# A hybrid encoder on one Trainium2 core: ten raw-weight buffers in the down-projection's first halves, and one more seven-product unit per layer

## Chip, cores and metric

The kernel runs on one core of one Trainium2 chip. The metric is the device time of one execution in microseconds (us); lower is better. A core has five engines that matter here: TensorE (PE; its weight loads are shown apart, as PEld) for matmuls, VectorE (DVE), ScalarE (ACT) and GpSimd (POOL) for elementwise work, and SyncE (SP), which issues nearly all the loads. Each engine works through its own instructions in order. All data are float32.

## The reference

An encoder of two layers over 256 positions of width 2048. Layer 0 has grouped-query attention with rotary positions, layer 1 three groups of dilated sliding-window attention. Either is followed by a gated feed-forward block with a depthwise convolution of width 3, which is what the change is about:

```
def conv_ffn(h, w_up, conv_w, conv_b, w_down):
    u = h @ w_up                                   # [256, 2048] @ [2048, 11264]
    u = lax.conv_general_dilated(u, ...) + conv_b  # depthwise, over positions, width 3
    gate, val = jnp.split(u, 2, axis=-1)           # 5632 columns each
    return (jax.nn.silu(gate) * val) @ w_down      # [256, 5632] @ [5632, 2048]

for i in range(DEPTH):                             # DEPTH = 2
    h = h + mixer(rms_norm(h, mix_norm[i]))
    h = h + conv_ffn(rms_norm(h, ffn_norm[i]), w_up[i], conv_w[i], conv_b[i], w_down[i])
return rms_norm(h, final_norm)
```

## The kernel before

**Split products.** To keep float32 accuracy on PE, each operand is split into a rounded high part and the rest: for a weight tile `raw`, ACT makes `wh` (a rounding copy) and DVE makes `wl = raw - wh`. A product is three matmuls, high by high, high by low and low by high (lines 160 to 162). The activations are the stationary operand, the weights stream through.

**An ordinary step, `feed`.** The weights lie in DRAM as blocks of 512 rows by 512 columns. `feed` takes one such block (a `kg`, 1 MB): it issues two loads of 512 KB (line 150), each into a raw buffer of 128 x 1024, splits each (lines 171 and 172) into a pair of buffers wh and wl, and issues 24 matmuls of 128x512, 12 per raw buffer. The split is given a priority 60 instructions ahead of its place (`AHEAD`), so that it runs ahead of the matmuls; which instruction of an engine comes when is fixed when the program is built.

**The seven-product unit, `fast_unit`.** For two column blocks n0 and n1 at the same kg, the work is a product of 2 x 2 blocks: two halves of the positions by two halves of the 512 rows, times those by two column blocks. Eight block products are done as seven (a scheme of the Strassen kind), 42 matmuls in place of 48 (lines 212 to 214). For that DVE makes four sums of weights (line 204), and seven weight tiles are split (lines 205 and 206) in place of four. The sums of activations are made once per kg and kept in `picks`. The accumulators of seven products are then folded into the four wanted ones: in the up-projection by lines 594 to 604, eight operations of 128x512 on DVE and one copy on ACT.

**Buffers.** `raw_tile` hands out raw buffers: four (`NRAW`) with tag raw, and, where `extra` is set, every third one from two further buffers with tag raw2, six in all. `new_split` hands out wh and wl: four pairs (`NHL`), and while `more` is set (in the up-projection behind a half's first pair) every third one from h0 and h1, two tiles of 8 KB per partition that hold the residual at other times and are parked in DRAM during most of the feed-forward block. SP issues the loads in order; a load waits until its raw buffer has been read by DVE.

**The feed-forward block, `ffn`.** The 5632 gate and 5632 value columns are worked in 11 pairs of a 512-column gate block and a value block, in two halves: pairs 0 to 5, then the down-projection of those (this document calls it the first half of the down-projection), then pairs 6 to 10 and the rest. A pair runs over four kgs. Pairs listed in `UP` (2, 4, 6 and 8) go through `up_pair`, with kg 0 as a seven-product unit in the order `UP_ORDER`; the others through `project`, gate first. The picks for kg 0 are made behind pair 0 (and for the second half from sums begun in the down-projection). Behind a pair come evacuation (ACT, line 539), a transposition (DVE line 427, POOL and ACT line 679), convolution (lines 659 and 667), silu, the product (703) and the split of the result (744, 745, or `combined` for kgs 1 and 2, which the down-projection takes in seven-product units). These are generators that `step` advances between the matmuls of `feed`; for pairs in UP the gate's generator goes into the list `beside`, which is advanced at other places of `feed` than the list `pending`.

**The down-projection's first half.** `pair` runs twice, for column blocks (0, 1) and (2, 3), each over six kgs in the order 0, 0, 3, 3, 4, unit 1, 4, 5, unit 2, 5: eight feeds and two units. The sums of weights for its units go into the u tiles of the convolution (`spot`), and results are added to the parked residual in DRAM.

Of the kernel before, what the change touches and what calls it, by code (L numbers as in the profile page):

```python
# [8 lines left out]
F32 = mybir.dt.float32  # L9
# [5 lines left out]
P = 128  # L15
# [7 lines left out]
SCALE = 128.0 ** -0.5  # L23
NRAW, NHL = 4, 4
AHEAD = 60
UP = 2, 4, 6, 8
MIX = (0, 1), (0, 2), (1, 1), (1, 2)
MIX_ORDER = (1, 0), (2, 0), (3, 0), (1, 1), (2, 1), (0, None), (3, 1)
EVEN = range(0, 16, 2)
# [7 lines left out]
def tile_encoder(ctx: ExitStack, tc: tile.TileContext, x, xT, w_a, w_ao, q_gain, k_gain, w_b, w_bo,  # L37
# [5 lines left out]
    hpool = ctx.enter_context(tc.tile_pool(name="hpool", bufs=1))  # L43
    spool = ctx.enter_context(tc.tile_pool(name="spool", bufs=1))
# [13 lines left out]
    h = {}  # L58
# [4 lines left out]
    def nm(s):  # L63
        uid[0] += 1
        return f"{s}_{uid[0]}"
# [58 lines left out]
            if len(pending) > keep:  # L124
                step()

    extra, count = [None], [0]

    def raw_tile():
        count[0] += 1  # L130
        if extra[0] and count[0] % 3 == 0:
            pool, tags = extra[0]
            tags.append(tags.pop(0))
            return pool.tile([P, 2, 512], F32, tag=tags[0], name=nm("raw"), bufs=2 if len(tags) == 1 else 1)
        return spool.tile([P, 2, 512], F32, tag="raw", name=nm("raw"), bufs=NRAW)
# [214 lines left out]
    def project2(w, n0, n1, lhs, kgs, late, first_done, hook=None, cuts=(), drained=()):  # L350
        a0, a1 = new_acc(), new_acc()
        cuts = (0, *cuts, len(kgs) - late, len(kgs))
        for c0, c1 in zip(cuts, cuts[1:]):
            part, end = range(c0, c1), c1 == len(kgs)
            if end:
                drain()
                for gen in drained:
                    start(gen())
            for accs, n in ((a0, n0), (a1, n1)):
                for i in part:  # L360
                    kg = kgs[i]
                    mid = hook and hook(n == n0, kg)
                    feed(accs, lhs, kg, w[n, kg], i == 0, i == len(kgs) - 1,
                         pieces=4 if hook and i < 2 else 2 if hook else 1, mid=mid)
                if end and n == n0:
                    first_done(a0)
        return a1
# [239 lines left out]
    def ffn(l, hT, ss_in, cw, g_next, last, side=None):  # L607
        with tc.tile_pool(name=nm("fpool"), bufs=1) as fp:
# [63 lines left out]
            def turned(s, u, at_once=False):  # L672
                quad = quad_tile(fp, "quad", 2)
                for m in range(2):
                    quad_T(quad, slice(m, 8, 2), s[:, m])

                def move(i, put):
                    q, c = QC[i]
                    put(u[32 * c:32 * c + 32, :, :, 32 * q:32 * q + 32],  # L679
                        quad[32 * q:32 * q + 32, c].rearrange("p (j m) t -> p j m t", m=2))  # L680

                for i in range(0, 16, 2):
                    move(i, nc.gpsimd.tensor_copy)
                if not at_once:
                    yield
                for i in range(1, 16, 2):
                    move(i, partial(nc.scalar.activation, func=AF.Copy))

            def gate_gen(accs, blk, value):
                s = evac_scaled(fp, accs, rstd, 1)  # L690
                yield
                yield from turned(s, blk[1])
                if value is not None:
                    for _ in range(1 if blk[0] not in UP else 4 if value[5] // 4 - 1 in fast else 3):
                        yield
                    with tc.issue_after(evac[0].ins):
                        nc.scalar.activation(value[3], value[3], AF.Silu)
                    yield from product(value)
# [6 lines left out]
            def value_gen(accs, blk, gate, last):  # L705
# [10 lines left out]
                yield from turned(s, blk[1])  # L716
                wait = 5 if last is None or gate[0] + 1 in UP else 4 if gate[0] in UP else 2
                if gate[0] + 1 in UP and last is not None and last[5] // 4 in fast:
                    for _ in range(wait):
# [70 lines left out]
            for hf, (p0, p1) in enumerate(HALVES):  # L790
# [5 lines left out]
                for p in range(p0, p1):  # L796
# [5 lines left out]
                    def gate_done(accs, gate=gate, last_value=last_value):  # L802
                        gen = gate_gen(accs, gate, last_value)
                        if gate[0] in UP:
                            next(gen)
# [7 lines left out]
                    if p == 0:  # L813
                        va = project2(w_up[l], 0, NPAIR, hT, kgs, 1, gate_done, None, (), [first])
                    elif p in UP:
                        va = up_pair(w_up[l], (p, NPAIR + p), hT, UP_ORDER, picks, junk, st_tile, gate_done)
# [92 lines left out]
                both = {kg: [(kg, 0), (kg, 1)] for kg in rest}  # L909
                f0, f1 = ([(kg, None)] for kg in fast)  # L910
                if hf == 0:
                    for ns in (0, 1), (2, 3):
                        if ns[0] == 2:
                            early = [fp.tile([P, 4, NT], F32, tag=t, name=nm(t)) for t in ("cg", "cv")]
                            start(sums_begun(hT, 0, *early, 4))
                        pair(wd, ns, slots, both[0] + both[3] + [(4, 0)] + f0 + [(4, 1), (5, 0)] + f1 + [(5, 1)], spot, folds,
                             None, 3 * (ns[0] == 0), ready)
                    continue
                accs = new_acc()
                for kg in range(np_):  # L920
# [725 lines left out]
```

## Time and profile before

| | |
|---|---|
| median of three timed runs | 2223.69 us (2222.29 to 2225.51) |
| profiled execution | 2221.27 us |
| its span, first to last instruction | 2219.5 us |
| PE busy | 2206.1 us (99%), 9933 matmuls |
| DVE busy | 1809.3 us (82%) |
| ACT busy | 1522.7 us (69%) |
| POOL busy | 543.5 us (24%) |
| granted clock of PE | 0.999 |
| read from HBM, written to it | 436.54 MB, 13.73 MB |

A row of the timeline has the start, the length, the engine, the line of the kernel, the operation, what it writes and reads, the shapes and the count; a bracket behind it says how long the engine stood idle before it and what ended that. A row of a group has the count, then the busy time, the mean length in ns of one, the idle time of the engine just before its members, and what ended it. Matmuls are pipelined: the length of one is longer than the distance to the next.

Where things lie in this execution: layer 0's pairs 0 to 5 from 257 to 516 us, its first half of the down-projection from 516 to 642; in layer 1 from 1505 to 1764 and from 1764 to 1891.

### The profile page before, as it was taken

How to read it: one execution, taken by the hardware profiler on the slowest of the kernel's cores; microseconds unless marked ns; L12 is line 12 of the kernel's file. 1: busy time of each engine (PE TensorE's matmuls, PEld its weight loads, DVE VectorE, ACT ScalarE, POOL GpSimd, SP SyncE). 2: the span in 40 equal slices, each digit the busy share in tenths (PEclk: the TensorE clock that was granted, in tenths of full speed). 3: DMA queues.
4: the chain of work that ended last, by engine and by line, in shares of the span. 5: the costliest groups of instructions: out<-in, count | busy, mean ns of one | idle time of the engine just before them, and what ended most of it. 6: DMA issues, size and time to landing. Idle time of an engine off the chain costs nothing.

```text
span 2219.5 us, 29025 instructions
## 1 busy us (share of the span) xinstructions
PE 2206.1 (99%) x9933; PEld 1829.4 (82%) x9933; DVE 1809.3 (82%) x2279; ACT 1522.7 (69%) x2328; POOL 543.5 (24%) x809
## 2 busy tenths in 40 slices
PE   9999999999999999999999999999999999999998
PEld 7888888888888888888888888888888888888887
DVE  6877768898887897978876878688798898879887
ACT  7666777787457787677756775567777855577754
POOL 3343221321002121041354216003222200212211
PEclk9999999999999999999999999999999999999999
DMA  8666765565767566666566555667565567756754
GB/s 302 193 221 201 240 205 181 192 200 188 216 209 237 184 203 224 206 202 199 180 202 197 171 184 187 192 203 242 168 219 190 189 202 212 238 173 209 255 191 142
DMA packets 129510, 452.19 MB, mean 204 GB/s; under 512 B 14665, under 2 KB 18505, under 8 KB 128337
## 3 DMA queue, kind: packets, MB, share of 16 engines
q1 hardware_dynamic: 123056, 429.05, 58.7%
q0 software_dynamic: 6016, 20.98, 3.9%
q8 instruction: 78, 1.28, 0.2%
q14 instruction: 72, 0.58, 0.1%
q10 hardware_dynamic: 288, 0.30, 0.0%
HBM read 436.54 MB, written 13.73 MB: 203 GB/s over the span
## 4 chain that ended last, share of the span: by engine, by line
PE 94%; DVE 2%; DMA 1%; issue 1%; POOL 1%; ACT 1%; SPq 0%; DVEq 0%; POOLq 0%; ACTq 0%
PE acc L161 27%; PE acc L160 27%; PE acc L162 27%; PE ps L213 2%; PE ps L212 2%; PE ps L214 2%; PE acc L213 2%; PE acc L214 2%; PE acc L212 2%; DVE wl L172 1%; DMA raw<-in_w_a_dram 1%; DMA raw<-in_w_down_dram 0%; PE ps L393 0%; PE ps L392 0%; DVE wl L206 0%
## 5 line engine op out<-in xcount | busy, mean ns | idle before, releaser
L172 DVE TENSOR_TENSOR wl<-raw,wh 128x1024 fp32r<-128x1024 f32 (+1 forms) x612 | 747.4, 1231 | 208.8 <-ACT wh L171 205.0
L171 ACT ACTIVATE wh<-raw 128x1024 fp32r<-128x1024 f32 (+1 forms) x612 | 633.5, 1044 | 277.6 <-PE acc L162 178.9
L160 PE MATMUL acc<-wh,xh 128*128 128x512 f32 x1632 | 636.7, 391 | 0.8 <-ACT wh L171 0.8
L161 PE MATMUL acc<-wl,xh 128*128 128x512 f32 x1632 | 636.1, 390 | 0.8 <-DVE wl L172 0.8
L162 PE MATMUL acc<-wh,xh 128*128 128x512 f32 x1632 | 634.8, 389 | 0.0
L679 POOL COPY u<-quad 32x256 f32<-32x256 f32 x352 | 223.5, 635 | 663.5 <-DVE quad L427 645.4
L161 PEld LDWEIGHTS acc<-wl,xh 128*128 128x128 f32 x1632 | 306.5, 188 | 64.4 <-DVE wl L172 2.7
L160 PEld LDWEIGHTS acc<-wh,xh 128*128 128x128 f32 x1632 | 306.5, 188 | 64.0 <-ACT wh L171 1.2
L162 PEld LDWEIGHTS acc<-wh,xh 128*128 128x128 f32 x1632 | 306.4, 188 | 63.9
L160 PE MATMUL acc<-wh,a 128*128 128x512 f32 x720 | 280.9, 390 | 0.0
L161 PE MATMUL acc<-wl,a 128*128 128x512 f32 x720 | 280.2, 389 | 0.0
L162 PE MATMUL acc<-wh,a 128*128 128x512 f32 x720 | 279.7, 389 | 0.0
L205 ACT ACTIVATE wh<-raw 128x1024 fp32r<-128x1024 f32 x128 | 135.7, 1060 | 116.0 <-PE acc L162 92.0
L679 ACT ACTIVATE u<-quad 32x256 f32<-32x256 f32 x352 | 147.8, 420 | 38.9 <-DVE quad L427 34.5
L206 DVE TENSOR_TENSOR wl<-raw,wh 128x1024 fp32r<-128x1024 f32 x128 | 154.2, 1222 | 12.0 <-ACT wh L205 11.4
L162 PEld LDWEIGHTS acc<-wh,a 128*128 128x128 f32 x720 | 135.1, 188 | 28.5 <-DVE a L378 0.2
L160 PEld LDWEIGHTS acc<-wh,a 128*128 128x128 f32 x720 | 135.2, 188 | 27.6
L161 PEld LDWEIGHTS acc<-wl,a 128*128 128x128 f32 x720 | 135.2, 188 | 27.4
L172 DVE TENSOR_TENSOR w<-raw,w 128x1024 fp32r<-128x1024 f32 x88 | 110.3, 1253 | 41.6 <-ACT w L171 41.6
L160 PE MATMUL acc<-w,xh 128*128 128x512 f32 x352 | 136.9, 389 | 0.0
L162 PE MATMUL acc<-w,xh 128*128 128x512 f32 x352 | 136.9, 389 | 0.0
L161 PE MATMUL acc<-w,xh 128*128 128x512 f32 x352 | 136.9, 389 | 0.0
(358 smaller groups left out, 3066.5 us busy)
## 6 DMA issues: line engine op xcount, KB each, us to landing
raw<-in_w_up_dram SPq DMA_DIRECT2D x352, 512.0 KB, 4.8
raw<-in_w_down_dram SPq DMA_DIRECT2D x176, 512.0 KB, 4.7
raw<-in_w_b_dram SPq DMA_DIRECT2D x144, 512.0 KB, 4.7
raw<-in_w_bo_dram SPq DMA_DIRECT2D x48, 512.0 KB, 4.3
raw<-in_w_a_dram SPq DMA_DIRECT2D x40, 512.0 KB, 4.7
raw<-in_w_ao_dram SPq DMA_DIRECT2D x32, 512.0 KB, 4.7
raw<-in_w_a_dram SPq DMA_DIRECT2D x16, 256.0 KB, 5.8
away<-h POOLq DMA_DIRECT2D x4, 1024.0 KB, 5.8
```

Source lines behind the costliest of these rows:

```text
L160: nc.tensor.matmul(accs[m], xh, wh[:, j, :], start=st, stop=False)
L161: nc.tensor.matmul(accs[m], xh, wl[:, j, :], start=False, stop=False)
L162: nc.tensor.matmul(accs[m], xl, wh[:, j, :], start=False, stop=sp)
L171: nc.scalar.activation(wh[:, c], r[:, c], AF.Copy)
L172: newest[0] = nc.vector.tensor_tensor(wl[:, c], r[:, c], wh[:, c].bitcast(F32), ALU.subtract)
L205: nc.scalar.activation(wh, r, AF.Copy)
L206: newest[0] = nc.vector.tensor_tensor(wl, r, wh.bitcast(F32), ALU.subtract)
L212: nc.tensor.matmul(acc[q], a, wh[:, j], start=st, stop=False)
L213: nc.tensor.matmul(acc[q], a, wl[:, j], start=False, stop=False)
L214: nc.tensor.matmul(acc[q], b, wh[:, j], start=False, stop=sp)
L679: put(u[32 * c:32 * c + 32, :, :, 32 * q:32 * q + 32], quad[32 * q:32 * q + 32, c].rearrange("p (j m) t -> p j m t", m=2))
```

## The change

Two edits. `UP` gets pair 1, so that pairs 1 and 2 of the first half of each layer are both run by `up_pair`. And in the first half of the down-projection `raw_tile` goes round ten buffers in a fixed order of five places: raw, raw2, raw, and two halves of h0 or h1 in turn. The counter of the ring is set to 0 at its start, so that the first h tile (h0) is asked for by the fourth load.

```
-UP = 2, 4, 6, 8
+UP = 1, 2, 4, 6, 8
...
-    extra, count = [None], [0]
+    extra, count, wide_ring, bits = [None], [0], [False], []
 
     def raw_tile():
         count[0] += 1
+        if wide_ring[0]:
+            if count[0] % 5 in (1, 3):
+                return spool.tile([P, 2, 512], F32, tag="raw", name=nm("raw"), bufs=NRAW)
+            if count[0] % 5 in (4, 0):
+                if not bits:
+                    t = hpool.tile([P, 4, 512], F32, tag=f"h{count[0] // 5 % 2}", name=nm("raw"))
+                    bits[:] = t[:, :2], t[:, 2:]
+                return bits.pop(0)
+            pool, tags = extra[0]
+            return pool.tile([P, 2, 512], F32, tag=tags[0], name=nm("raw"), bufs=2)
         if extra[0] and count[0] % 3 == 0:
...
                 if hf == 0:
+                    wide_ring[0], count[0] = True, 0
                     for ns in (0, 1), (2, 3):
...
                         pair(wd, ns, slots, both[0] + both[3] + [(4, 0)] + f0 + [(4, 1), (5, 0)] + f1 + [(5, 1)], spot, folds,
                              None, 3 * (ns[0] == 0), ready)
+                    wide_ring[0] = False
+                    bits.clear()
                     continue
```

In the texts below, "pair two" is the second pair (number 1 in the code), "pair three" the third (number 2), and so on.

## The prediction

> **What bounds the kernel now.** I read the profile's page first, then what TensorE (PE) waited for, then the timeline of PE.
>
> ```profile
> span 2219.5 us, 29025 instructions
> ...
> PE 2206.1 (99%) x9933; PEld 1829.4 (82%) x9933; DVE 1809.3 (82%) x2279; ACT 1522.7 (69%) x2328; POOL 543.5 (24%) x809
> ```
>
> PE is busy for 2206.1 of 2219.5 us, so 13.4 us is all the idle time there is. The view of PE's waits shows how little of it has a cause that could be removed:
>
> ```profile
> PE ps L393 <- DVE qTl L378: 2.0, 1, 2.0
> PE ps L499 <- DVE warm L496: 1.5, 1, 1.5
> PE acc L160 <- ACT wh L171: 0.8, 1, 0.8
> PE acc L161 <- DVE wl L172: 0.8, 3, 0.3
> PE acc L213 <- DVE wl L206: 0.8, 1, 0.8
> ```
>
> Five lines, 5.9 us. The kernel takes as long as its matmuls take one behind the other, and two things alone can shorten it: fewer matmuls, or the last few stalls. What a matmul is worth is read from the timeline of PE in the second gate/value pair of layer 0, where 36 matmuls lie from the first of these rows to the last:
>
> ```profile
> 319.61 0.39 PE L160 MATMUL acc<-wh,xh 128*128 128x512 f32 x1
> ...
> 327.77 0.39 PE L160 MATMUL acc<-wh,xh 128*128 128x512 f32 x1
> ```
>
> 8.16 us / 36 = 0.2267 us from start to start (the 0.39 is a pipelined duration and overlaps the next). The profiled execution took 2221.27 us, 1.8 above its span and 2.4 below the median of the three timed runs (2223.69). I make the sum as a difference and put it on the median. Of this kernel, some 0.2% (4.45 us) can be told from no change.
>
> **Part one: a seven-product unit in pair two.** An ordinary pair issues 192 matmuls: 2 blocks x 16 slices of 128 rows x 2 halves of the positions x 3. The unit takes 7 x 2 x 3 = 42 for what otherwise takes 48. Two layers save 12 matmuls: 12 x 0.2267 = 2.72 us, all of it on the bound engine.
> The Trainium skill, page "TensorE: Matmul & The Clock Gate", section "Back-to-back issue gap", gives about 216 ns for an isolated gap at 512 columns and about 131 ns for a sustained stream. By these, twelve matmuls would be worth an estimated 2.59 or 1.57 us; the trace's 226.7 ns agrees with neither figure and decides.
>
> What is added falls on DVE and ACT. These are the rows of the same operations where the kernel has them now:
>
> ```profile
> L206 DVE TENSOR_TENSOR wl<-raw,wh 128x1024 fp32r<-128x1024 f32 x128 | 154.2, 1222 | 12.0 <-ACT wh L205 11.4
> L204 DVE TENSOR_TENSOR raw<-raw,raw 128x1024 f32<-128x1024 f32 x62 | 76.9, 1241 | 0.8
> L596 DVE TENSOR_TENSOR fold<-ps,junk 128x512 f32<-128x512 f32 x12 | 8.1, 678 | 0.0
> L205 ACT ACTIVATE wh<-raw 128x1024 fp32r<-128x1024 f32 x128 | 135.7, 1060 | 116.0 <-PE acc L162 92.0 <-DVE raw L204 9.4 <-PE ps L214 7.5
> ```
>
> Seven splits in place of four: 3 x 1.22 = 3.7 us on DVE and 3 x 1.06 = 3.2 us on ACT. Four sums of weights: 4 x 1.24 = 5.0. The fold, lines 596 to 604: eight operations of 128x512 at 0.68, 5.4. DVE gets 14.1 us per layer. The sums of activations that the unit reads (picks) are made in pair one already, for the later pairs, so they cost nothing more. Is there room? The stretches of pairs two and three in layer 0 and of pair two in layer 1 (columns: length, then busy PE, PEld, DVE, ACT, POOL):
>
> ```profile
> 300.60:344.10 43.50, 43.50 (x194) 36.02 (x193) 31.32 (x40) 33.74 (x50) 9.66 (x18) 1.00 0.59 194
> 344.10:387.20 43.10, 43.10 (x191) 35.31 (x190) 37.82 (x48) 33.37 (x51) 9.72 (x16) 1.00 0.53 175
> 1549.00:1592.50 43.50, 43.50 (x194) 36.02 (x193) 31.23 (x40) 34.49 (x52) 10.44 (x20) 1.00 0.61 205
> ```
>
> Pair two leaves DVE idle for 12.2 us. It is to hold 14.1 more and is 6 x 0.2267 = 1.36 us shorter: 45.4 us of work in 42.1. With pair three, DVE has 83.2 us of work in 85.2. What hides the overflow is the lead of the splits over PE, so I measured it as the end of a split on DVE against the matmul that first reads its lower half, in layer 0:
>
> ```profile
> 340.00 1.23 DVE L172 TENSOR_TENSOR wl<-raw,wh 128x1024 fp32r<-128x1024 f32 x1
> 352.48 0.39 PE L161 MATMUL acc<-wl,xh 128*128 128x512 f32 x1
> 351.11 1.23 DVE L206 TENSOR_TENSOR wl<-raw,wh 128x1024 fp32r<-128x1024 f32 x1 [0.29 <-ACT wh L205]
> 360.64 0.39 PE L213 MATMUL ps<-wl,xh 128*128 128x512 f32 x1
> 365.79 1.22 DVE L172 TENSOR_TENSOR w<-raw,w 128x1024 fp32r<-128x1024 f32 x1
> 370.16 0.39 PE L161 MATMUL acc<-w,xh 128*128 128x512 f32 x1
> ```
>
> The lead is 352.48 - 341.23 = 11.3 us late in pair two, 8.3 at the first split of pair three's own unit, and 3.2 just behind that unit: a unit eats five. Coming into pair three 3.3 us poorer (45.4 against 42.1), the lead behind its unit is 3.2 - 3.3, about nothing. So PE stalls from 0 to some 1 us per layer there; I take 0.4, 0.8 for both, near the row. The far end is the slower rival below. ACT goes to 33.7 + 3.2 = 37 of 42.1 us and is not late.
>
> **Part two: ten raw buffers in the first halves of the down-projection.** How much does PE lose there? A first half issues 2 x (8 x 24 + 2 x 42) = 552 matmuls, and these rows are the first matmul of it and the first behind it, in layer 0:
>
> ```profile
> 516.45 0.39 PE L160 MATMUL acc<-wh,a 128*128 128x512 f32 x1
> 642.03 0.39 PE L160 MATMUL acc<-wh,xh 128*128 128x512 f32 x1
> ```
>
> and in layer 1:
>
> ```profile
> 1763.77 0.39 PE L160 MATMUL acc<-wh,a 128*128 128x512 f32 x1
> 1890.59 0.39 PE L160 MATMUL acc<-wh,xh 128*128 128x512 f32 x1
> ```
>
> 552 x 0.2267 = 125.12 us; the stretches last 125.58 and 126.82. The stalls are 0.46 + 1.70 = 2.16 us, the most that part two can give. Do they come from the loads? The largest of them, with DVE ahead of it (a bracket is idle time and what ended it):
>
> ```profile
> 1807.32 1.23 DVE L204 TENSOR_TENSOR u<-raw,raw 128x1024 f32<-128x1024 f32 x1 [4.02 <-DMA raw<-in_w_down_dram]
> ...
> 1811.87 2.48 DVE L204 TENSOR_TENSOR u<-u,raw 128x1024 f32<-128x1024 f32 x2
> 1814.26 1.22 DVE L206 TENSOR_TENSOR wl<-raw,wh 128x1024 fp32r<-128x1024 f32 x1
> 1815.54 0.50 PE L213 MATMUL acc<-wl,s 128*128 128x512 f32 x1 [0.77 <-DVE wl L206]
> ```
>
> The first sums of the units, grouped over each of the two first halves (layer 1, then layer 0; the last column is DVE's idle time before them):
>
> ```profile
> L204 DVE TENSOR_TENSOR u<-raw,raw 128x1024 f32<-128x1024 f32 x4 | 4.9, 1226 | 12.1 <-DMA raw<-in_w_down_dram 12.1
> L204 DVE TENSOR_TENSOR u<-raw,raw 128x1024 f32<-128x1024 f32 x4 | 4.9, 1226 | 11.3 <-DMA raw<-in_w_down_dram 11.3
> ```
>
> DVE waits 4.0 us for a load, does the sums in a row, is late with the third split by a hair, and PE stalls. The load was late because six buffers are in use and a unit holds four until its sums are done. With ten, the sums go into that idle time, and the late split comes up to 4 us earlier than its reader needs. Units that follow another closely gain most; the first unit of each half waited only about 1 us for a load and has its small stall from other work. I take 1.7 of the 2.16; ends 0 and 2.16.
>
> Two transfers are moved past a new wait. The fourth and fifth loads go into h0, which the up-projection uses for split weights, so SP holds them, and every load behind them, until PE has read that tile for the last time:
>
> ```profile
> raw<-in_w_down_dram SPq DMA_DIRECT2D x176, 512.0 KB, 4.7
> ```
>
> Counting the calls of new_split through the changed program, the last split in h0 is the sixth from the end of the up-projection in layer 0 and the third from the end in layer 1. One split is 12 matmuls, 2.72 us. In layer 1 the load can go 2 x 2.72 = 5.4 us ahead of the end, lands 0.7 ahead of it, and is split 1.06 + 1.22 later, at +1.6; PE wants it behind three loads, at 3 x 2.72 = +8.2. 6.6 us are to spare, more in layer 0: nothing. At the other end the normal ring is back before h0 and h1 serve the splits again. No matmul, sum or byte is added by part two.
>
> **The sum.** -2.72 + 0.8 - 1.7 = -3.6 us: 2223.69 - 3.6 = 2220.1 us (the profiled execution: 2217.7).
>
> **Rivals.**
> (a) *Everything comes.* No new stall, and all 2.16 us back: -2.72 - 2.16 = -4.9, 2218.8 us, just past what can be told. For it: the small size of every cost, and that ten buffers give DVE 23.4 us (12.1 + 11.3) of waiting back. Against it: 83.2 of 85.2 us.
> (b) *The ring does nothing.* Then the change does not do what its words say: DVE's order is fixed at build time, and if the two sums stay just ahead of the third split (the 2.48 us row above), the stall stays although the loads are early. -2.72 + 0.8 = -1.9, 2221.8 us.
> (c) *DVE becomes the bound in pairs two and three.* The idle time of pair two may not be usable:
>
> ```profile
> L172 DVE TENSOR_TENSOR wl<-raw,wh 128x1024 fp32r<-128x1024 f32 x12 | 14.7, 1237 | 6.8 <-ACT wh L171 6.7
> L171 ACT ACTIVATE w<-raw 128x1024 fp32r<-128x1024 f32 x5 | 5.3, 1055 | 3.3 <-PE acc L162 3.3
> ```
>
> More than half of it is DVE waiting for ACT's half of a split, and only some of ACT's waits are for PE (buffers full, a true reserve). With none of the 12.2 us used, the overflow is 14.1 + 1.36 - 8.3 (the lead at pair three's unit) = 7.2 us per layer: -2.72 - 1.7 + 14.3 = +9.9, 2233.6 us. Slower by over 0.2% needs 4.4 us of stall per layer, so DVE would have to use less than 14.1 + 1.36 - 8.3 - 4.4 = 2.8 of the 12.2 us. Against it: behind its unit in pair three DVE already runs with no idle at all, so ACT can run ahead of a late DVE.
> The same page of the Trainium skill, section "The HAM clock gate", says that PE's clock halves after an idle window of about 3.4 us; the longest wait above is 2.0, so no trace here shows it.
>
> **How the numbers follow.** The forecast 0.42, (a) 0.26, (b) 0.23, (c) 0.09. Faster by over 0.2% is (a): 0.26; slower is (c): 0.09; within, 0.65. The range goes from (a) less the scatter of the timed runs (1.5) at 2217.3 to part of the way into (c) at 2226.0, which leaves out less than 2 in 10.
>
> **What would show it.** Right: 9921 matmuls; in pair two of both layers DVE busy near 42 us; fewer than 1.5 us of PE stalls around pair three's unit; in the first halves of the down-projection DVE's waits for loads in front of its first sums down from 23.4 us to under 8, and stretches under 125.6 us. Wrong: those waits gone and the stalls there as before, which is (b); or PE waiting for splits (L160, L161, L213) for over 4 us between pair two and pair four of a layer, which is (c).

## The result, and the profile after

The changed kernel takes 2227.36 us (median of 20 runs, 2225.54 to 2230.58) against 2223.65 for the kernel before, measured beside it (20 runs, 2221.03 to 2226.24): a ratio of 1.0020, 95% interval 1.0013 to 1.0026. The forecast was 2220.1 us and the range ended at 2226.0, so the sign was wrong and the time lies outside the range. Measured a second time (run 7 below), the ratio was 1.0019 (1.0010 to 1.0027).

The page of the changed kernel, for the two lines shown of before:

```profile
span 2227.3 us, 29037 instructions
...
PE 2207.4 (99%) x9921; PEld 1827.3 (82%) x9921; DVE 1837.9 (83%) x2309; ACT 1529.4 (69%) x2336; POOL 563.0 (25%) x809
```

The 12 matmuls are gone (9921) and the span is 7.8 us longer all the same. What took their place stands in the view of PE's waits (all lines are ten higher than before: 223 was 213, 171 was 161):

```profile
PE ps L223 <- DVE wl L216: 3.2, 5, 0.9
PE ps L403 <- DVE qTl L388: 2.0, 1, 2.0
PE acc L223 <- DVE wl L216: 1.7, 2, 1.0
...
PE acc L171 <- DVE wl L182: 1.3, 4, 0.5
PE acc L171 <- DVE w L182: 1.1, 2, 0.8
```

Four of the five are waits for DVE's half of a split; before, such waits came to 1.6 us in all (the rows of L161 and L213 in the prediction). Where? I cut PE's matmuls into stages and took from each stage's length (its first matmul to that of the next stage) the number of its matmuls x 0.22665 us; stages in which PE never waits come out at 0.00 with that spacing. Pair three of layer 1, and the two first halves of the down-projection, from their first row to the first row behind them:

```profile
1593.97 0.39 PE L170 MATMUL acc<-wh,xh 128*128 128x512 f32 x1
...
1640.69 0.39 PE L170 MATMUL acc<-w,xh 128*128 128x512 f32 x1
```

```profile
517.23 0.39 PE L170 MATMUL acc<-wh,a 128*128 128x512 f32 x1
...
644.43 0.39 PE L170 MATMUL acc<-wh,xh 128*128 128x512 f32 x1
...
1770.43 0.39 PE L170 MATMUL acc<-wh,a 128*128 128x512 f32 x1
...
1898.51 0.39 PE L170 MATMUL acc<-wh,xh 128*128 128x512 f32 x1
```

46.72 - 186 x 0.22665 = 4.56 us of stalls in pair three of layer 1. Before had none there (42.16 us for the same 186 matmuls):

```profile
1592.41 0.39 PE L160 MATMUL acc<-wh,xh 128*128 128x512 f32 x1
...
1634.57 0.39 PE L160 MATMUL acc<-w,xh 128*128 128x512 f32 x1
```

The first halves last 127.20 and 128.08 us for 552 x 0.22665 = 125.11: 2.09 and 2.97, where before had 0.46 and 1.71. With 0.79 and 0.55 in the two pairs four, the sum over the profile is -2.72 (matmuls) + 5.86 (pairs three and four) + 2.89 (first halves) + 2.5 (in the attention of both layers; the last section tells of 1.6 of it) = +8.5, for a span that grew by 7.8 (0.15 came back in the two pairs seven and about 0.6 in the first 9 us). A second profiled execution of the same kernel (run 7 below) had 2.69 in place of 4.56 and no such loss in layer 0's attention: +4.3 us, near the +3.7 of the medians.

Pair three of layer 1 from near, in the timeline:

```profile
1615.76 1.22 DVE L216 TENSOR_TENSOR wl<-raw,wh 128x1024 fp32r<-128x1024 f32 x1
...
1616.89 1.22 DVE L214 TENSOR_TENSOR raw<-raw,raw 128x1024 f32<-128x1024 f32 x1
...
1617.03 0.50 PE L223 MATMUL ps<-wl,s 128*128 128x512 f32 x1 [0.95 <-DVE wl L216]
...
1618.03 1.22 DVE L216 TENSOR_TENSOR w<-raw,w 128x1024 fp32r<-128x1024 f32 x1
...
1619.30 0.50 PE L223 MATMUL ps<-w,s 128*128 128x512 f32 x1 [0.62 <-DVE w L216]
```

A split ends at 1616.98 and PE takes it at 1617.03; the next ends at 1619.25 and is taken at 1619.30. The lead of the splits is 0.05 us, DVE has no bracket, and PE goes as fast as DVE makes a sum and a split: DVE is the bound here. The busy times of the same three stretches as in the prediction (columns: length, then PE, PEld, DVE, ACT, POOL):

```profile
301.96:344.12 42.16, 42.16 (x188) 34.91 (x187) 38.54 (x45) 34.54 (x50) 12.83 (x18) 1.00 0.55 188
344.12:387.24 43.12, 43.12 (x191) 35.32 (x190) 41.92 (x52) 34.69 (x55) 13.29 (x16) 1.00 0.51 166
1551.81:1593.97 42.16, 42.16 (x188) 34.91 (x186) 34.58 (x37) 31.64 (x49) 13.79 (x19) 1.00 0.54 176
```

Pair two did not take its share: DVE is busy for 38.5 us there in layer 0 and 34.6 in layer 1, where the prediction had some 42. Of the rest, 4.1 us fall into layer 0's pair three (41.9 us for 37.8 before). In layer 1 part of the idle time is a wait for a load:

```profile
1581.67 1.06 ACT L181 ACTIVATE wh<-raw 128x1024 fp32r<-128x1024 f32 x1 [5.30 <-DMA raw<-in_w_up_dram]
...
1582.76 1.23 DVE L182 TENSOR_TENSOR wl<-raw,wh 128x1024 fp32r<-128x1024 f32 x1 [3.96 <-ACT wh L181]
```

The other part, the ring of ten, did to the loads what it was to do. The first sums of the units, grouped over each first half (layer 0, then layer 1):

```profile
L214 DVE TENSOR_TENSOR u<-raw,raw 128x1024 f32<-128x1024 f32 x4 | 4.9, 1224 | 2.8 <-DMA raw<-in_w_down_dram 2.8
L214 DVE TENSOR_TENSOR u<-raw,raw 128x1024 f32<-128x1024 f32 x4 | 4.9, 1224 | 3.9 <-DMA raw<-in_w_down_dram 3.9
```

DVE waits 6.7 us for loads in front of them, where it waited 23.4. And PE stalls more. The first unit of layer 0's first half shows why:

```profile
544.63 2.48 DVE L214 TENSOR_TENSOR u<-u,raw 128x1024 f32<-128x1024 f32 x2
...
547.03 1.22 DVE L216 TENSOR_TENSOR wl<-raw,wh 128x1024 fp32r<-128x1024 f32 x1
...
548.31 0.50 PE L223 MATMUL acc<-wl,s 128*128 128x512 f32 x1 [0.77 <-DVE wl L216]
...
550.98 1.23 DVE L214 TENSOR_TENSOR u<-raw,raw 128x1024 f32<-128x1024 f32 x1 [0.46 <-DMA raw<-in_w_down_dram]
...
552.12 2.35 DVE L216 TENSOR_TENSOR wl<-u,wh 128x1024 fp32r<-128x1024 f32 x2
...
553.40 0.50 PE L223 MATMUL ps<-wl,s 128*128 128x512 f32 x1 [0.70 <-DVE wl L216]
```

The two sums still stand ahead of the third split (first stall), and the first sum of the *next* unit, whose loads the ring lets come early, now stands ahead of this unit's last two splits (second stall). Run 4 below asks whether this order is the cause.

### The profile page after: what moved, and what is told of

It reads as the page before. It is cut to its first block, busy times and chain, and to the rows that moved or that the text cites. A ratio compares the mean times of both kernels' runs of the same rounds, so it can differ in the third digit from the quotient of the medians.

```text
span 2227.3 us, 29037 instructions
## 1 busy us (share of the span) xinstructions
PE 2207.4 (99%) x9921; PEld 1827.3 (82%) x9921; DVE 1837.9 (83%) x2309; ACT 1529.4 (69%) x2336; POOL 563.0 (25%) x809
## 4 chain that ended last, share of the span: by engine, by line
PE 49%; DVE 3%; DMA 2%; issue 1%; ACT 1%; POOL 1%; DVEq 0%; POOLq 0%; ACTq 0%
PE acc L171 14%; PE acc L172 14%; PE acc L170 14%; PE ps L223 1%; PE ps L224 1%; PE ps L222 1%; PE acc L223 1%; PE acc L224 1%; PE acc L222 1%; DVE wl L182 1%; DMA raw<-in_w_up_dram 1%; DVE wl L216 1%; DMA raw<-in_w_down_dram 1%; ACT wh L181 0%; DMA raw<-in_w_b_dram 0%
## 5 line engine op out<-in xcount | busy, mean ns | idle before, releaser
L182 DVE TENSOR_TENSOR wl<-raw,wh 128x1024 fp32r<-128x1024 f32 (+1 forms) x606 | 741.5, 1234 | 204.5 <-ACT wh L181 201.0
L181 ACT ACTIVATE wh<-raw 128x1024 fp32r<-128x1024 f32 (+1 forms) x606 | 626.4, 1044 | 289.5 <-PE acc L172 186.4
L171 PE MATMUL acc<-wl,xh 128*128 128x512 f32 x1608 | 627.7, 390 | 1.4 <-DVE wl L182 1.3
L170 PE MATMUL acc<-wh,xh 128*128 128x512 f32 x1608 | 627.9, 391 | 0.9 <-ACT wh L181 0.9
L172 PE MATMUL acc<-wh,xh 128*128 128x512 f32 x1608 | 626.2, 390 | 0.0
L689 POOL COPY u<-quad 32x256 f32<-32x256 f32 x352 | 244.9, 696 | 646.0 <-DVE quad L437 628.0
L170 PEld LDWEIGHTS acc<-wh,xh 128*128 128x128 f32 x1608 | 302.4, 188 | 63.0 <-ACT wh L181 1.4
L172 PEld LDWEIGHTS acc<-wh,xh 128*128 128x128 f32 x1608 | 302.2, 188 | 62.6
L215 ACT ACTIVATE wh<-raw 128x1024 fp32r<-128x1024 f32 x138 | 146.0, 1060 | 110.1 <-PE acc L172 84.7
L216 DVE TENSOR_TENSOR wl<-raw,wh 128x1024 fp32r<-128x1024 f32 x138 | 168.3, 1234 | 25.5 <-ACT wh L215 24.5
L171 PE MATMUL acc<-w,xh 128*128 128x512 f32 x344 | 134.1, 390 | 1.1 <-DVE w L182 1.1
L172 PE MATMUL acc<-w,xh 128*128 128x512 f32 x344 | 133.9, 389 | 0.0
L170 PE MATMUL acc<-w,xh 128*128 128x512 f32 x344 | 133.8, 389 | 0.0
```

Of the source, the lines that this page charges most:

```text
L170: nc.tensor.matmul(accs[m], xh, wh[:, j, :], start=st, stop=False)
L171: nc.tensor.matmul(accs[m], xh, wl[:, j, :], start=False, stop=False)
L172: nc.tensor.matmul(accs[m], xl, wh[:, j, :], start=False, stop=sp)
L181: nc.scalar.activation(wh[:, c], r[:, c], AF.Copy)
L182: newest[0] = nc.vector.tensor_tensor(wl[:, c], r[:, c], wh[:, c].bitcast(F32), ALU.subtract)
L215: nc.scalar.activation(wh, r, AF.Copy)
```

## The experiments

Theory A: the lead of the splits over PE is a stock. A unit takes more of DVE than it takes of PE, so it draws on the stock; what it lacks is a stall, there or at the next unit, however far. Theory B, over the runs in several forms: the loads, or the mere order on DVE, make the splits late. Stalls in us, by the reckoning above (pairs: two to six of a half, without 0.97 us in layer 0's pair three, which in every kernel are mostly four small matmuls of another kind and no stall); the leads are from the end of a split to the first matmul that reads its lower half, at the first split of the stage.

| kernel | ratio to before (95%) | pairs, layer 0 / 1 | first halves, layer 0 / 1 | lead into layer 1's pair two | lead into layer 0's first half |
|---|---|---|---|---|---|
| before | 1 | 0.04 / 0.00 | 0.46 / 1.71 | 7.8 | 6.2 |
| changed | 1.0020 (1.0013 to 1.0026) | 0.79 / 5.11 | 2.09 / 2.97 | 5.1 | 4.4 |
| 1 unit only | 1.0008 (0.9999 to 1.0017) | 0.04 / 1.04 | 2.61 / 0.16 | 7.0 | 4.7 |
| 2 ring only | 1.0003 (0.9995 to 1.0012) | 0.03 / 0.00 | 0.66 / 2.32 | 6.3 | 6.2 |
| 3 counter kept | 1.0005 (0.9996 to 1.0014) | 0.70 / 2.21 | 2.36 / 1.67 | 7.2 | 4.4 |
| 4 sums in order | 1.0016 (1.0007 to 1.0025) | 0.17 / 1.90 | 1.87 / 2.39 | 6.3 | 4.4 |
| 5 POOL sums, pair two | 1.0062 (1.0049 to 1.0074) | 4.66 / 8.44 | 2.14 / 2.45 | 4.8 | |
| 6 units apart | 1.0027 (1.0016 to 1.0039) | 0.03 / 0.00 | 4.56 / 2.64 | 4.7 | 2.3 |
| 7 changed, again | 1.0019 (1.0010 to 1.0027) | 0.34 / 2.98 | 2.18 / 2.42 | 5.6 | 4.4 |
| 8 POOL sums, all | 1.0422 (1.0408 to 1.0436) | 12.5 / 15.2 | 16.0 / 14.0 | | |
| 9 no folds | 0.9999 (0.9990 to 1.0008) | 0.03 / 1.36 | 0.40 / 1.82 | 6.5 | 6.2 |
| 10 no sums | 1.0009 (1.0000 to 1.0018) | 0.05 / 0.00 | 2.08 / 2.29 | 4.1 | 4.4 |
| 11 six splits | 0.9993 (0.9985 to 1.0002) | 0.03 / 0.00 | 0.11 / 0.01 | 7.6 | 7.5 |
| 12 unit, six splits | 0.9990 (0.9981 to 0.9999) | 0.57 / 0.71 | 0.47 / 0.01 | 7.1 | 5.6 |
| 13 unit, shifted | 1.0022 (1.0013 to 1.0031) | 0.56 / 4.58 | 4.36 / 1.91 | 4.9 | 4.0 |
| 14 apart, six splits | 1.0016 (1.0008 to 1.0025) | 0.03 / 0.00 | 3.38 / 3.22 | 7.5 | 4.5 |

**1 and 2: either part alone.** The kernel before with one of the two edits.

```
-UP = 2, 4, 6, 8
+UP = 1, 2, 4, 6, 8              # run 1; run 2 has the ring and the old UP
```

> The added unit alone, with the ring of before. The changed kernel lost 5.05 us in layer 1 around pair three's unit and only 0.2 us at that place in layer 0, and in layer 1 the splits' lead was already 3 us lower than before when pair two began. Theory A: the ring did that, by setting the counter of raw_tile to 0 in layer 0, which shifts the place of the raw2 buffers in the round of three for everything behind it. Then here, with the counter as before, layer 1's lead at the start of pair two is 8 to 10 us as before, its stall around pair three is under 1 us, and the time is 1 to 2 us below before (ratio 0.9990 to 0.9998). Theory B: the 14.1 us that DVE gets in pair two are the cause, with any ring: a stall of 4 to 5 us in layer 1 here too, and a ratio of 1.0005 to 1.0015.

> The ten buffers alone, with UP as before (9933 matmuls). Theory A: the ring is no gain by itself. In DVE's order the second and third sum of each first unit still stand ahead of the third split, and the next unit's first sum now stands ahead of the last two splits, so that the first unit of each half keeps a stall of about 1 us and gets a second one of up to 0.9, while the stalls of the later units go: the two first halves lose 1.5 to 3 us in all (before: 2.16), ratio 0.9995 to 1.0005. Theory B: the stalls there in the changed kernel (4 us in all) come only from the poorer lead that pair two's unit leaves behind: here under 0.7 us in both first halves, ratio 0.9988 to 0.9995.

The unit alone stalls PE little in the pairs (1.0 us), about as theory A had it, but brings 2.15 more in layer 0's first half, where no edit was made; layer 1's first half has 1.55 less, and why it has is open. By the stages that is -2.72 + 1.0 + 2.15 - 1.55 = -1.1 us, but the medians show no gain (A's ratio was missed): a ratio of 0.9995 lies outside the interval, so one profile does not hold all of it. The ring alone gains nothing although it takes the waits for loads away. Neither alone makes the 5.1 us of layer 1's pairs; that takes both.

**3 and 4: the ring's counter, and the order of the sums.** Run 3 gives the counter of raw buffers back behind the ring as it would have been; run 4 ties each sum to the split made ahead of it.

```
-                    wide_ring[0], count[0] = True, 0
+                    wide_ring[0], kept, count[0] = True, count[0], 0
...
-                    wide_ring[0] = False
+                    wide_ring[0], count[0] = False, kept + count[0]
```

```
-                    nc.vector.tensor_tensor(*sums[q], ALU.add)
+                    with tc.issue_after(newest[0].ins) if wide_ring[0] else ExitStack():
+                        nc.vector.tensor_tensor(*sums[q], ALU.add)
```

> Both parts as changed, but the ring gives the counter of raw_tile back as it would have been (its value at the start plus 48), so that the round of three behind it has the phase of before. Theory A (the shifted phase makes layer 1's 5 us): that stall falls under 1 us, and the time falls by about 4 us against the changed kernel, to a ratio of 0.9995 to 1.0005. Theory B (the phase has nothing to do with it): 1.0015 to 1.0025 as the changed kernel, and a stall of 4 to 5 us at the same place.

> Both parts as changed, but in the first halves of the down-projection each sum of weights is held behind the split before it in program order on DVE, so that no sum stands ahead of an earlier split. Theory A (DVE's order makes the stalls there): the two first halves, which lost 4 us in the changed kernel, lose under 1 us; the rest is unchanged, so the ratio is 1.0000 to 1.0010. Theory B (DVE is simply late there, whatever the order): 3 to 5 us of stalls in them, ratio 1.0015 to 1.0025.

Keeping the counter lifts the lead into layer 1's pair two from 5.1 to 7.2 us, and the stalls of its pairs are 2.2 us (5.1 and, in run 7, 3.0 with the reset); theory A had expected under 1 in pair three, which kept 1.7. Ordering the sums does not help: in the first halves 4.3 us stay, in other places. So the order alone is not the cause there: in layer 0 DVE has no idle time from 525.3 to 555.9 us in run 4, whatever comes first. That part of the theory fell. What the order does without the new unit was not run.

**5 and 8: the sums on POOL.** Meant to take 4.6 us per unit from DVE.

```
-                    nc.vector.tensor_tensor(*sums[q], ALU.add)
+                    nc.gpsimd.tensor_tensor(*sums[q], ALU.add)    # run 5: in pair two's unit only
```

> The changed kernel, with the four sums of weights of pair two's unit made by POOL and not by DVE. Theory A (the lead of the splits over PE is a stock: a unit with its 7 splits and 4 sums takes some 12.5 us of DVE in 9.5 us of PE, and two units in neighbouring pairs drain it): DVE gets 4 x 1.14 = 4.6 of the 14.1 us back. PE's stalls in pair three of layer 1 fall from 4.56 us to under 1, those in pair four of layer 0 from 0.79 to under 0.2, those in the first half of the down-projection of layer 0 from 2.09 to under 1.3; ratio 0.997 to 0.9995. Theory B (the 10 us without a load behind a unit in pair two, and the burst behind it, are the cause, since the unit holds four of six raw buffers until its sums are made): POOL takes at least 2.2 us a sum (1.10 for 128x512), so the buffers are held longer, the stretch without a load grows, and layer 1's pair three keeps 3 us or more; ratio 1.001 or more.

> The changed kernel, with the four sums of weights of every unit made by POOL. Theory A: DVE, which is what comes late, gets 4.6 us back for every unit; no stall over 0.5 us in a pair of gates and values, under 1 us in each first half of the down-projection; ratio 0.997 to 0.9985. Rival: three of the four sums of a unit hang on one another, POOL takes 2.2 to 3.9 us for each (two times 1.10 to 1.96 for 128x512), and in the down-projection the splits lead by 2 to 6 us only; PE then waits 1 us or more for each of its units, and the ratio is over 1.002.

Both are slower, run 8 by 4%. The timeline of run 5, in pair two's unit, shows that this did not relieve DVE:

```profile
308.23 5.76 POOL L214 TENSOR_TENSOR raw<-raw,raw 128x1024 f32<-128x1024 f32 x2
...
308.48 3.23 DVE L216 TENSOR_TENSOR wl<-raw,wh 128x1024 fp32r<-128x1024 f32 x1 [1.49 <-ACT wh L215]
...
311.63 3.43 DVE L216 TENSOR_TENSOR w<-raw,w 128x1024 fp32r<-128x1024 f32 x1
314.02 1.06 ACT L215 ACTIVATE wh<-raw 128x1024 fp32r<-128x1024 f32 x1 [2.29 <-POOL raw L214]
```

A split that takes DVE 1.22 us elsewhere takes 3.2 to 3.4 beside a POOL sum. POOL's sum is slower too (2.9 us each here, 1.24 on DVE), and ACT waits for it. Over run 8 (groups; count, busy us, mean ns of one):

```profile
L216 DVE TENSOR_TENSOR wl<-raw,wh 128x1024 fp32r<-128x1024 f32 x138 | 261.2, 1911 | 50.1 <-ACT wh L215 48.3
```

1911 ns for 1234 in the changed kernel: 138 x 0.677 = 93 us more of DVE in this group alone. The Trainium skill, page "SBUF — State Buffer", section "Who interferes with whom", says that a DVE instruction with two inputs in SBUF contends with a POOL instruction that reads SBUF. These rows agree: DVE's two splits stretch over POOL's two sums. So neither run decides between A and B; the expected gain of run 5 went into longer splits and the wait for slower sums, and how much into each was not taken apart.

**6: the units apart.** As many matmuls, sums and folds as in the changed kernel, in pairs two, four and six.

```
-UP = 1, 2, 4, 6, 8
+UP = 1, 3, 5, 6, 8
```

> The changed kernel, with the three units of each layer's first half in pairs two, four and six, where it has them in two, three and five: as many matmuls, sums and folds, but no two units in neighbouring pairs. Theory A (a stock that two neighbouring units drain): under 0.5 us of stalls in pairs two to five of both layers (the changed kernel: 0.8 and 5.1); the third unit is now next to the down-projection, whose first unit finds less lead: 4 to 6 us in the two first halves together (5.1). Ratio 0.998 to 1.0005. Rival, the sum of DVE's work decides, not the distance: the lead falls from unit to unit, with more than 1.5 us of stalls by pairs four to six of each layer; ratio 1.001 or more.

In the pairs A is right to the letter: 0.03 and 0.00. But the down-projection pays 4.56 + 2.64, more than forecast, since the third unit stands right in front of it and its first splits lead by 2.3 us. The ratio was forecast at 0.998 to 1.0005 and came out at 1.0027: the stock is drawn on from both sides of that border.

**7: the changed kernel once more.**

> The changed kernel once more, unaltered, with a profile of its own. Theory A: its stalls come from the order and the work of DVE, so they come again: pair three of layer 1 4 to 5 us, first halves of the down-projection 2.0 to 2.2 and 2.8 to 3.1; ratio 1.001 to 1.0025. Rival: the 4.56 us of layer 1 hang on when loads happened to land in that one execution, and this one shows under 3 us there, with the first halves as before.

The first halves come nearly again (2.18 for 2.09, 2.42 for 2.97); pair three of layer 1 does not (2.69 for 4.56). The rival holds in so far: there the size of the stall goes with when loads land. In the first profile ACT waited 5.3 us for one, in this one 3.9; the lead at the unit was 3.0 us there and 3.7 here.

**9 and 10: what of the new unit costs.** Run 9 leaves out the eight folding operations of pair two (lines 604 to 614 but for the copy), run 10 its four sums.

```
+            if ns[0] == 1:
+                first_done((a2, a4))
+                continue
             with tc.issue_after(newest[0].ins):
                 tt(v, acc[6], a, ALU.subtract)
...
+        if ns[0] == 1:
+            return a3, a8
         tt(a3, a3, v, ALU.add)
```

```
-                if q in sums:
+                if q in sums and not bare[0]:
```

> The changed kernel; pair two leaves out the eight DVE operations that fold its unit's products into the accumulators (its gates and values are then those of the plain products alone). Loads, splits and sums stay as they are. Theory A (what DVE has to do there drains the lead of the splits): 8 x 0.68 = 5.4 us of DVE less per layer, so the stalls in pair three of layer 1 (4.56 and 2.69 us in two executions) fall under 0.5, those of pair four of layer 0 under 0.1, and the first half of the down-projection in layer 0 under 1.5 (2.1 to 2.2); ratio 0.9985 to 1.0005. Theory B (the 10 to 12 us without a load behind the unit in pair two, and the burst that lands late): the gap is there as before, and layer 1 keeps over 2 us in pair three.

> The changed kernel; pair two's unit leaves out its four sums of weights (its products take the weights themselves). Folds, splits and loads stay. Theory A: 4 x 1.24 = 5.0 us of DVE less per layer, and the stalls go as they go without the folds: pair three of layer 1 under 0.5 us, pair four of layer 0 under 0.1. Theory B: the raw buffers come free earlier, the gap in the loads shrinks by 3 us or more, and the stalls go here but stayed without the folds. Ratio 0.9985 to 1.0005 with both.

In layer 0's first half the folds are the whole cost. Without them it has 0.40 in place of 2.09, with the ring still in place (pair four, 130 us earlier, has 0.03):

```profile
514.01 0.39 PE L170 MATMUL acc<-wh,a 128*128 128x512 f32 x1
...
639.52 0.39 PE L170 MATMUL acc<-wh,xh 128*128 128x512 f32 x1
```

125.51 - 125.11 = 0.40. Without the sums pair four's stall goes as well (0.05), but the first half keeps its 2.08, against A's expectation that the two would do the same. The timeline shows a reason. Inside the unit DVE would else wait for ACT's half of the splits: from 308 to 322 us its waits for ACT are 1.9 us in the changed kernel and 6.9 in run 10, one of them

```profile
311.04 1.23 DVE L216 TENSOR_TENSOR wl<-raw,wh 128x1024 fp32r<-128x1024 f32 x1 [1.42 <-ACT wh L215]
```

so the four sums fill time that DVE would have idled. The folds come behind the unit, six of the eight at 322 to 332 us, the last of these

```profile
331.38 0.68 DVE L612 TENSOR_TENSOR fold<-ps,fold 128x512 f32<-128x512 f32 x1
```

and two at 346 to 347; from 322 to 353 us DVE is idle for 0.5 us only. So what the folds take is missing behind them. In layer 1 either helps: 0.00 without the sums, 1.36 without the folds, between what A (under 0.5) and B (over 2) expected. Without the sums the raw buffers come free earlier, and the stretch in which SP issues no load behind the unit shrinks from 10.2 us (1558.85 to 1569.09) to 7.3; without the folds it stays at 10.2. So the late loads behind the unit have a part in layer 1, and DVE's work has one. By themselves the late loads stall nothing: run 14 below has them in layer 1 too (12.0 us without a load, then up to 8.0 us to landing) and 0.00 in its pairs, where no unit follows in pair three. Run 10's ratio (1.0009) is above the 1.0005 that both theories had.

**11 and 12: a deeper lead in place of earlier loads.** h0 and h1 as a fifth and a sixth split buffer in the first halves, not as raw buffers; run 12 also has the unit in pair two.

```
-                more[0] = False
+                more[0] = hf == 0
                 start(flush(last_value))
...
                         pair(wd, ns, slots, ...)
+                    more[0] = False
                     continue
```

> The kernel before, without the new unit and without ten raw buffers; the two tiles h0 and h1 serve in the first halves of the down-projection as a fifth and a sixth split buffer, as they do in the up-projection. Theory A (there the lead is capped by four split buffers, 5.9 us at the most, and is at 0.1 us by the third product of a unit; loads are not what is late): the lead in front of a unit goes over 7 us, and the stalls of the two first halves (0.46 + 1.71) fall under 0.4 together; ratio 0.9987 to 0.9997. Rival (the loads are late, as the prediction had it): with six raw buffers as before DVE waits for loads as long, over 18 us ahead of the first sums of both halves, and over 1.5 us of stalls stay; ratio 0.9997 to 1.0005.

> The kernel before with the unit in pair two and with the two more split buffers in the first halves of the down-projection (in place of the ten raw buffers). Theory A (the new unit's cost is paid out of a lead, and where the lead has been refilled or is deep enough it costs nothing): pairs three and four as with the unit alone (1.1 us), the two first halves under 1 us together (2.8 with the unit alone); 12 matmuls less: ratio 0.9980 to 0.9993. Rival: the lead that is missing at the entry of the down-projection (4.4 us for 6.2) stalls PE all the same, over 1.5 us in the first half of layer 0; ratio 0.9995 to 1.0005.

Run 11 in layer 1: the first sums of its units, and the stretch.

```profile
L204 DVE TENSOR_TENSOR u<-raw,raw 128x1024 f32<-128x1024 f32 x4 | 4.9, 1223 | 9.4 <-DMA raw<-in_w_down_dram 9.4
```

```profile
1765.89 0.39 PE L160 MATMUL acc<-w,a 128*128 128x512 f32 x1
...
1891.01 0.39 PE L160 MATMUL acc<-wh,xh 128*128 128x512 f32 x1
```

DVE waits 9.4 us for loads (12.1 before), and PE stalls for 125.12 - 125.11 = 0.01 us (1.71 before). The waits that the ring was to remove cost nothing; what was short was the depth of the lead. The ratio of run 11 is 0.9993, with 1 in the interval. Run 12 saves the 12 matmuls, 2.72 us, and pays 1.6 of that in stalls that run 11 has not (1.2 in the pairs, 0.4 in the first halves). Its ratio, 0.9990 (0.9981 to 0.9999), is the one here whose interval lies below the kernel before, and is below that of the changed kernel by about 0.3%; from run 11 it cannot be told.

**13: the numbering alone.** Run 1 with the counter of raw buffers one higher behind each first half, as the ring's reset leaves it.

```
+                    count[0] += 1
                     continue
```

> The kernel before with the unit in pair two alone, and one change of numbering: behind the first half of each down-projection the counter of raw buffers is one higher, as the reset to 0 leaves it in the changed kernel (48 for 224, the remainder by 3 one higher). No ring of ten. Theory A (layer 1 comes poorer into pairs two and three since the two extra raw buffers of the pools take other loads there; with the unit in pair two alone the splits lead by 7.0 us at the start of layer 1's pair two, with the counter reset by 4.1 to 6.5): the lead there falls under 6.6 us, and the stalls of pair three of layer 1 rise from 0.36 us to 1.5 or more; layer 0 as with the unit alone (0.04 in pair four, 2.6 in the first half). Ratio 1.0005 to 1.0025. Rival (the ring itself, through the bursts of loads and the order on DVE, makes layer 1 poorer): lead 7.0, stalls under 0.6 us.

A's expectation holds in layer 1. The first split of pair two, and the matmul that reads it, in run 1 and in run 13:

```profile
1544.25 1.22 DVE L172 TENSOR_TENSOR wl<-raw,wh 128x1024 fp32r<-128x1024 f32 x1
...
1552.46 0.39 PE L161 MATMUL acc<-wl,xh 128*128 128x512 f32 x1
```

```profile
1548.99 1.23 DVE L172 TENSOR_TENSOR w<-raw,w 128x1024 fp32r<-128x1024 f32 x1 [1.75 <-ACT w L171]
...
1555.10 0.39 PE L161 MATMUL acc<-wl,xh 128*128 128x512 f32 x1
```

The lead is 7.0 us in the one and 4.9 in the other, and the stalls of pair three go from 0.36 to 3.68 (those of pair four from 0.68 to 0.90). So the numbering alone, with no ring and no other edit, lowers the lead there. Over all kernels that holds: the lead into layer 1's pair two is 4.1 to 6.5 us where the counter was shifted and 7.0 to 7.8 where not. It reaches further too: with four split buffers the lead into layer 1's first half is 6.2 us without the shift and 4.2 to 4.9 with it (run 8 apart; 4.7 in run 2, which has no new unit). The stalls say less, since single profiles scatter: in layer 0, where run 13's edit does not act yet, it has 0.56 and 4.36 us for run 1's 0.04 and 2.61; and in layer 1's pairs run 4, with the shift, has 1.90 and run 3, without, 2.21. The medians go the same way as the lead (1.0008 without the shift, 1.0022 with it).

**14: apart, with six split buffers.** Run 12 with the units in pairs two, four and six.

```
-UP = 1, 2, 4, 6, 8
+UP = 1, 3, 5, 6, 8
```

> The kernel before with three units in each layer's first half, in pairs two, four and six, and with six split buffers in the first halves of the down-projection (no ring of ten). Theory A (units apart cost nothing in the pairs; what the last one lacks at the entry of the down-projection is 4.6 and 2.6 us of stalls with four split buffers, and with six the first unit there has 3 to 4 us more lead): no stall over 0.1 us in pairs two to six, under 2 us in the two first halves together; ratio 0.9978 to 0.9992. Rival (the debt of the last unit stalls PE before the deeper lead is built up): over 3 us in the two first halves; ratio 0.9995 to 1.001.

The rival was right: 3.4 and 3.2 us. More buffers deepen the lead only where DVE has idle time to fill them, and in front of the down-projection's first unit it has next to none: in layer 0 it is busy for 34.65 of the 35 us from 505 to 540, in run 12 for 31.3.

## Why the prediction was wrong

**The price of PE's work: right.** 9921 matmuls, 12 x 0.2267 us.

**The new stalls, 0.8 us for both layers: the step that failed.** "Coming into pair three 3.3 us poorer (45.4 against 42.1), the lead behind its unit is 3.2 - 3.3, about nothing. So PE stalls from 0 to some 1 us per layer there." In layer 0's pairs that is about what happened: the lead just behind that unit fell to 1.1 us, and pair four stalls 0.79 and 0.34 us in the two profiles. It failed in two ways.
- *It took layer 1 to be layer 0.* The leads were read in layer 0 alone. Before the change the lead into pair two was 11.3 us there and 7.8 in layer 1. The other part of the change, whose raw counter starts at 0, lowers it in layer 1 (runs 3 and 13), and loads behind the unit land late (runs 7 and 10). Pair three's unit found 3.0 and 3.7 us of lead where the step reckoned with 8.3 - 3.3 = 5.0. The stalls in layer 1's pairs were 5.11 and 2.98. By the prediction's own sign (over 4 us between pairs two and four) the first is rival (c), with its mechanism: of pair two's idle time a part was not to be used, since DVE stayed idle for 7.6 of 42.2 us there.
- *It closed the account at pair four.* What is missing need not be made good by the plain pairs in between (in layer 1 with the unit alone it was: 6.2 us at the entry). At the entry of layer 0's first half the splits still lead by 1.8 us less (before, then changed: 516.68 - 510.46 = 6.2 and 517.46 - 513.07 = 4.4):

```profile
509.24 1.22 DVE L172 TENSOR_TENSOR wl<-raw,wh 128x1024 fp32r<-128x1024 f32 x1
...
516.68 0.39 PE L161 MATMUL acc<-wl,a 128*128 128x512 f32 x1
```

```profile
511.85 1.22 DVE L182 TENSOR_TENSOR wl<-raw,wh 128x1024 fp32r<-128x1024 f32 x1
...
517.46 0.39 PE L171 MATMUL acc<-wl,a 128*128 128x512 f32 x1
```

The first unit there had no reserve before the change either (its third product's split led by 0.1 us in the kernel before, by the same reckoning), so a missing 1.8 us became 1.63 us of stalls. Run 9 shows that the folds of pair two, some 200 us earlier, are what is paid there.

**The ring, -1.7 us: mis-read as a wait that costs.** "With ten, the sums go into that idle time, and the late split comes up to 4 us earlier than its reader needs." The waits went (23.4 to 6.7 us, the sign that the prediction asked for) and no stall with them: the first halves have 0.66 + 2.32 with the ring alone, 2.17 before. Rival (b) was right in what came out. Its mechanism, the two sums ahead of the third split, stands in the timeline, but run 4, which puts the sums behind, moves the stalls and does not remove them. So the order is not shown as the cause; run 11 shows that the depth of the lead is. What the prediction left out is that early loads also let the next unit's sum go ahead, and that the shifted counter takes 1.5 us of lead from layer 1's first half: with the ring and the counter kept (run 3) that half stalls 1.67 us, as before the change (1.71). The idle time of DVE in front of a sum was read as the cause of a late split; run 11 keeps most of that idle time (20.1 us over both layers) and has no stall.

**The sum.** -2.72 stayed; 0.8 became 5.9 (first profile) or 3.3 (second); -1.7 became +2.9 or +2.4. That a slower kernel had a chance of 0.09 came from pricing (c) as all or nothing in both layers, while a part of it in one layer, with a ring that costs, was enough.

**Open:** by what path the numbering costs layer 1 its 1.5 to 3 us of lead (which load goes into which buffer is all that was changed); and of the 4.56 us in the first profile, how much is the late load alone (the second execution has 1.9 less).

## What to carry to other kernels

Treat the lead of a preparing engine over the bound engine as an account with one balance over the whole program, and look up the balance at its lowest point before adding work anywhere upstream: a debt was paid here some 200 us behind the work that made it. An engine's wait for a load is a cost only if the work behind it reaches its reader late; a deeper buffer between the engines (split buffers) removed stalls that an earlier load (raw buffers) did not. Any edit that shifts the turn of a rotating buffer also changes code far behind it, so price it there too, layer by layer.

## What the runs showed of the hardware

**PE at half rate behind a wait of 2 us.** Run 13, first unit of layer 0's first half (timeline, then two windows, around the wait and behind it; the third column from the right is PE's granted clock):

```profile
548.62 0.39 PE L212 MATMUL acc<-wh,s 128*128 128x512 f32 x1
550.86 0.50 PE L213 MATMUL acc<-wl,s 128*128 128x512 f32 x1 [1.85 <-DVE wl L206]
...
552.44 0.63 PE L212 MATMUL ps<-wh,s 128*128 128x512 f32 x1
552.86 0.63 PE L213 MATMUL ps<-wl,s 128*128 128x512 f32 x1
```

```profile
548.60:551.60 3.00, 1.15 (x5) 0.64 (x4) 3.00 (x3) 1.06 (x1) 0.00 (x0) 1.00 0.29 90
551.80:555.10 3.30, 3.30 (x10) 2.55 (x9) 3.30 (x4) 1.06 (x1) 0.00 (x0) 0.50 0.77 262
```

Matmuls start 0.43 us apart for about 3 us (the trace has the clock at 0.50 for 3.41 us), which costs 1.6 us on top of the wait, and 1.6 of run 13's 4.36. The same follows the wait for `qTl` at 144 us (1.9 to 2.0 us) in the attention of layer 0 in 8 of the 16 profiles, the first of the changed kernel among them, and not in the others, where the wait is as long or up to 0.5 shorter. It is 1.6 of the 2.5 us by which the first profile of the changed kernel was longer in the attention; it says nothing of the change. The Trainium skill, page "TensorE: Matmul & The Clock Gate", section "The HAM clock gate", gives an idle window of about 3.4 us for this, with a window that runs free of the program; here an idle time of 1.85 us was enough at times, and the length of the slow stretch, 3.41 us, is the 3.4 us that it gives for the way back.

**Late loads.** A load of 512 KB lands 3.7 us after its issue when SP has issued none for a while; in the burst behind pair two's unit in layer 1 it took up to 7.9 us in the changed kernel and 8.1 in run 3.
